# Prompt attention beside the FFN's first part, FFN operand sums woven into the prompt's mixers and output projection, row tiles prepared one ahead

## The chip, the cores and the metric

The kernel runs on one core of a Trainium2 chip. The metric is the device time of one execution in microseconds. A core has TensorE (PE; its weight loads are shown as PEld), VectorE (DVE), ScalarE (ACT), GpSimd (POOL), and queues for transfers, of which SyncE's (SP) carries nearly all here. All matrix products are done on fp32 values split into a high and a low part of type fp32r, with three products (high x high, high x low, low x high) for one.

## The reference

One layer of a hybrid encoder trunk is applied to two sequences with the same weights: the sample (2048 tokens, "s") and the prompt (512 tokens, "p"), 1024 channels each.

```python
h = rms_norm(x, norm1_g)
p = h @ w_in                                   # 1024 -> 1792, split among three mixers
a = windowed_attention(q, k, v, ...)           # 8 heads of 64, 2 kv heads, blocks of 128, +-128 tokens, sink logit
b = multiscale_pool(pool_in, pool_w, pool_scale)   # means over 2/4/8/16 tokens minus token, group linear
c = hyena_mixer(hy_in, ...)                    # short conv, two gated FFT convolutions with implicit filters
cat = concat(rms_norm(a), rms_norm(b), rms_norm(c))
x = x + cat @ w_out
h = rms_norm(x, norm2_g)
u = dwconv3(h @ w_ffn_in, ...)                 # 1024 -> 2 x 2816, depthwise conv of width 3 over tokens
x = x + (gelu(u[..., :2816]) * u[..., 2816:]) @ w_ffn_out
```

## The kernel before

The program is written with a tile framework that inserts the waits and orders the instructions of each engine by its own estimate; the order in which the program issues them is the priority.

Issue order comes from generators. A "main" list and a "side" list of work are run by `drive`: each step of either yields its planned cost in nanoseconds of a planner's clock (`now`). For each cost of main, side may issue work up to `ratio` times that cost. A step that yields `None` waits for a due time (`until`) or for a result (`need`); side then yields to main. `T_NORM` (6500), `T_RMS`, `T_SM` and the like are planned latencies. What is left of side when main is over is issued alone. `weave(x, y)` issues one step of y after each step of x, then the rest of y.

The stages:

1. `front` (main): input projections of both sequences, then the sample's output projection, row tile by row tile (16 of 128 rows), to `x2["s"]` in DRAM. Beside it (side): filter spectra, the sample's pooling, Hyena and attention, then the prompt's attention, then `prep`, which builds `h0`, the normed, transposed and split first 512 rows of the sample (`ffn_prep`, transposes in line 360). Main ends with `need("h0")`.
2. `ffn_in` (main): the FFN's up-projection for these 512 rows, 22 pairs of column tiles, 16 steps of three 128x512 products each (lines 326 to 328, with the weights `fwhi`, `fwlo`). Beside it (side, after `need("up")`): the prompt's pooling and Hyena, its output projection `out_proj`, then `sums(0)` and `sums(1)`. From "up" on, the side work has the banks 4 to 7: attention's scores two (4, 5), its transposes one (6), its output one (7); before, five banks were theirs, two of them for transposes.
3. `ffn_in7` twice: the other 2048 rows in two groups of 1024, as seven products of half-size blocks in place of eight. It needs as operands sums and differences of the two row halves' blocks. `ffn_sums` makes them: per pair of row tiles a load, norm and transposes (line 1329) of two tiles, and sums into a tile `o` (seven blocks), stored to `ops[0]` or `ops[1]` in DRAM. `ffn_operands` loads each of the seven blocks through two `st` buffers, and splits it (ScalarE the high part, VectorE or GpSimd the low part). `sums(0)` takes rows of the sample alone; `sums(1)` pairs the sample's last 512 rows with the prompt's, and waits for each prompt row tile of x2.
4. `ffn_out`: the down-projection of all rows with all weights held in SBUF.

The prompt's `out_proj` works in two halves of 512 columns. In each half it loads that half of `w_out` (eight blocks, scaled and split), and for each of four row tiles loads the concatenated mixers `ca` and the residual, squares, splits and sums (`out_prep`), waits `T_NORM`, and multiplies. The sample's out projection in `front` already uses `out_product`, which does both halves of a row tile in one go.

The functions that the change touches:

Of the kernel before, what the change touches and what calls it, by code (L numbers as in the profile page):

```python
# [11 lines left out]
F32 = mybir.dt.float32  # L12
F32R = mybir.dt.float32r
AF = mybir.ActivationFunctionType
ALU = mybir.AluOpType
# [3 lines left out]
DM = 1024  # L19
KD = DM // 128  # L20
# [209 lines left out]
RATIOS = (1.0, 1.2, 0.8)  # L230
RATIO_P = 1.0
FH = 512
# [3 lines left out]
GROUPS = ((0, 4), (4, 6), (6, 8))  # L236
T_NORM, T_SIN, T_RMS, T_SM, T_PT, T_INV, T_CONV, T_EV, T_POOL, T_LOAD, T_FILL = 6500, 6000, 7000, 9000, 2500, 4500, 9000, 2500, 2500, 4200, 1300
# [5 lines left out]
class Trunk:  # L243
# [51 lines left out]
    def bank(self, i):  # L295
        return self.ps.tile([128, 512], F32, tag=f"b{i}", name=f"b{i}")
# [946 lines left out]
    def out_proj(self, s, bank, src, key):  # L1243

        nc, tc, d = self.nc, self.tc, self.d
        n, L = s.name, s.L
        with tc.tile_pool(name=f"outp{n}", bufs=1, side="right", reuse_waits="tile") as pool:
            for h in range(2):
                hs = slice(h * 512, h * 512 + 512)
                wo = {}  # L1250
                for k in range(KD):
                    raw = pool.tile([128, 512], F32, tag="raw", bufs=2, name="raw")
                    nc.sync.dma_start(out=raw, in_=d["w_out"][0, k * 128:k * 128 + 128, hs])
                    hi, lo = (pool.tile([128, 512], F32R, tag=f"ow{nm}{k}", name=f"ow{nm}{k}") for nm in ("hi", "lo"))
                    go = self.go[:, k:k + 1]
                    nc.scalar.activation(hi, raw, AF.Copy, scale=go)
                    nc.vector.scalar_tensor_tensor(lo, raw, go, hi.bitcast(F32), op0=ALU.mult, op1=ALU.subtract)
                    wo[k] = (hi, lo)
                    if h == 0:
                        yield from self.until(self.now + T_LOAD / 2)  # L1260
                yield from self.need((key, n))
                for t in range(L // 128):
                    ts = slice(t * 128, t * 128 + 128)
                    ca = pool.tile([128, DM], F32, tag="ca", bufs=2, name="ca").rearrange("p (k t) -> p k t", k=KD)
                    nc.sync.dma_start(out=ca, in_=self.cat[n][:, ts].rearrange("(k p) t -> p k t", p=128))
                    x = pool.tile([128, 512], F32, tag="ox", bufs=2, name="ox")
                    nc.sync.dma_start(out=x, in_=src[ts, hs])
                    sq = pool.tile([128, KD, 128], F32, tag="osq", name="osq")
                    hi, lo = (pool.tile([128, KD, 128], F32R, tag=nm, bufs=2, name=nm) for nm in ("chi", "clo"))
                    self.out_prep(ca, sq, hi, lo)  # L1270
                    yield from self.until(self.now + T_NORM)
                    r = self.out_scale(pool, bank, sq, GROUPS)
                    for i, (k0, k1) in enumerate(GROUPS):
                        ps = bank()
                        for k in range(k0, k1):
                            self.mm3(ps, hi[:, k], lo[:, k], wo[k][0], wo[k][1], k == k0, k == k1 - 1)
                            yield 650
                        nc.vector.scalar_tensor_tensor(x, ps, r[:, i:i + 1], x, op0=ALU.mult, op1=ALU.add)
                    nc.gpsimd.dma_start(out=self.x2[n][ts, hs], in_=x)
                    if h:  # L1280
                        self.done.add(("x2", n, t))


    def prep_rows(self, pool, tiles):
# [11 lines left out]
                yield from self.until(t)  # L1296
                yield x

    def ffn_prep(self, tiles, hi, lo, bank):

        with self.tc.tile_pool(name="ffp", bufs=1, side="right", reuse_waits="tile") as pool:
            i = 0
            for x in self.prep_rows(pool, tiles):
                if x is None or isinstance(x, (int, float)):
                    yield x
                    continue
                yield from self.norm_t(x, 128, hi, lo, i * 128, bank)
                i += 1

# [1 line left out]

    def ffn_sums(self, dst, tiles, bank):

        nc = self.nc
        with self.tc.tile_pool(name="ffs", bufs=1, side="right", reuse_waits="tile") as pool:
            i, o = 0, None  # L1320
            for x in self.prep_rows(pool, tiles):
                if x is None or isinstance(x, (int, float)):
                    yield x
                    continue
                pv = []
                for k0 in range(0, KD, 4):
                    ps = bank()
                    for k in range(k0, k0 + 4):
                        nc.tensor.transpose(ps[:, (k - k0) * 128:(k - k0) * 128 + 128], x[:, 128 * k:128 * k + 128], self.ident)  # L1329
                    pv.append(ps.rearrange("p (k t) -> p k t", k=4))  # L1330
                    yield 450
                if i % 2 == 0:
                    o = pool.tile([128, 7, 4, 128], F32, tag="o", name="o")
                    for j in range(2):
                        nc.scalar.activation(o[:, j], pv[j], AF.Copy)
                else:
                    nc.vector.tensor_tensor(o[:, 3], pv[0], o[:, 0], op=ALU.subtract)
                    nc.vector.tensor_tensor(o[:, 4], pv[1], o[:, 3], op=ALU.subtract)
                    nc.scalar.activation(o[:, 2], pv[1], AF.Copy)
                    nc.gpsimd.tensor_tensor(o[:, 5], o[:, 4], o[:, 0], op=ALU.subtract)  # L1340
                    nc.gpsimd.tensor_tensor(o[:, 6], o[:, 1], o[:, 4], op=ALU.subtract)
                    c = i // 2 * 128
                    nc.sync.dma_start(out=dst[:, :, :, c:c + 128].rearrange("p o k t -> p (o k) t"), in_=o.rearrange("p o k t -> p (o k) t"))
                i += 1

    def ffn_operands(self, pool, stage, src):

        h = {}
        for i, op in enumerate((0, 4, 5, 3, 1, 6, 2)):
            x = stage.tile([128, 4, FH], F32, tag="st", bufs=2, name="st")  # L1350
            self.nc.sync.dma_start(out=x, in_=src[:, op])
            h[op] = pool.tile([128, 2, 4, FH], F32R, tag=f"o{op}", name=f"o{op}")
            self.split(x, h[op][:, 0], h[op][:, 1], self.nc.gpsimd if i % 2 else None)
        return h

# [209 lines left out]
    def run(self):  # L1565
        tc, nc, d = self.tc, self.nc, self.d
        S, P = SEQS["s"], SEQS["p"]
        self.done, self.now, self.strict = set(), 0.0, False
        chain = itertools.chain
        c = self.ctx.enter_context(tc.tile_pool(name="const", bufs=1, reuse_waits="tile"))  # L1570
# [3 lines left out]
        def pooled(s, a):  # L1574
            with tc.tile_pool(name="pool" + s.name, bufs=2, side="right", reuse_waits="tile") as pool:
                yield from self.pooling(s, a, pool)
# [12 lines left out]
        att = [att(i) for i in range(3)]  # L1589


        h0 = []

        def prep():

            pool = mctx.enter_context(tc.tile_pool(name="h0", bufs=1, side="right", reuse_waits="tile"))
            h0.extend(pool.tile([128, KD, 512], F32R, name=f"h0{i}") for i in range(2))
            yield from self.ffn_prep([("s", t) for t in range(0, 512, 128)], *h0, a)
            self.done.add("h0")

        def sums(i):

            pairs = [[("s", 512 + t), ("s", 1024 + t)] if i == 0 else [("s", 1536 + t), ("p", t)] for t in range(0, FH, 128)]
            return self.ffn_sums(self.ops[i], [x for p in pairs for x in p], a)

        def consts():
            yield from self.until(START)
# [2 lines left out]
        def pace(r):  # L1610
            self.ratio = r
            return
            yield

        side = chain(consts(), pace(RATIOS[0]), self.spectra(S, a), self.spectra(P, a), pooled(S, a), pace(RATIOS[1]), self.hyena(S, [[0], [1]], a),
                     self.mark("c", "s"), pace(RATIOS[2]), self.attention(S, *att), self.attention(P, *att), prep(), self.need("up"),
                     pooled(P, a), self.hyena(P, [[0, 1]], a), self.mark("cat", "p"),
                     self.out_proj(P, a, d["x_p"][0], "cat"), sums(0), sums(1))

        side = self.drive(chain(self.front(), self.need("h0")), side, RATIO)  # L1620

# [5 lines left out]
        with (tc.tile_pool(name="hops", bufs=1, side="right", reuse_waits="tile") as hops,  # L1627
              tc.tile_pool(name="ffw7", bufs=1, reuse_waits="tile") as pool, tc.tile_pool(name="stage", bufs=1, reuse_waits="tile") as stage):
            fb = self.rotate(range(8))
            for i, parts in enumerate(([(S, 512, 1024)], [(S, 1536, 512), (P, 0, 512)])):  # L1630
                h = self.ffn_operands(hops, stage, self.ops[i])
# [36 lines left out]
```

## Time and profile before

| | |
|---|---|
| median of 3 runs | 3180.19 us (3179.9 to 3184.45) |
| profiled execution | 3178.09 us |
| its span, first to last instruction | 3176.3 us |
| mean granted TensorE clock | 0.98 |
| TensorE busy | 2977.4 us |
| VectorE / ScalarE / GpSimd busy | 1944.5 / 1320.5 / 596.8 us |

Lines "L326" and the like are lines of the program above; a line in a helper (the three products, the split) is shared by many callers, so that tile names tell them apart. Matmuls overlap, so a busy stretch is not necessarily a full one; PEclk is the share of the full clock that TensorE was granted. The span's middle has these marks: the prompt's attention begins at 1074 us, `ffn_in` at 1206 us, its last product is at 1586 us, and `ffn_in7` begins at 1634 us.

### The profile page before, as it was taken

How to read it: one execution, taken by the hardware profiler on the slowest of the kernel's cores; microseconds unless marked ns; L12 is line 12 of the kernel's file. 1: busy time of each engine (PE TensorE's matmuls, PEld its weight loads, DVE VectorE, ACT ScalarE, POOL GpSimd, SP SyncE). 2: the span in 40 equal slices, each digit the busy share in tenths (PEclk: the TensorE clock that was granted, in tenths of full speed). 3: DMA queues.
4: the chain of work that ended last, by engine and by line, in shares of the span. 5: the costliest groups of instructions: out<-in, count | busy, mean ns of one | idle time of the engine just before them, and what ended most of it. 6: DMA issues, size and time to landing. Idle time of an engine off the chain costs nothing.

```text
span 3176.3 us, 41398 instructions
## 1 busy us (share of the span) xinstructions
PE 2977.4 (94%) x15488; PEld 2475.9 (78%) x15488; DVE 1944.5 (61%) x3162; ACT 1320.5 (42%) x2235; POOL 596.8 (19%) x470
## 2 busy tenths in 40 slices
PE   7999999999999978999849999989999999999999
PEld 6888888888888767878637888868888867888887
DVE  7443576769998776665538888887777642111111
ACT  5223444458876554443433444444444432111110
POOL 1000000022242310011243444443233200000000
PEclk9999999999999998999969999999999999999999
DMA  5555576654433335654872222232222154223222
GB/s 176 149 154 145 163 214 188 184 157 117 132 106 95 118 107 159 197 180 140 241 216 93 80 80 80 83 123 88 84 81 80 61 168 146 73 73 100 73 74 76
DMA packets 438990, 401.40 MB, mean 126 GB/s; under 512 B 75961, under 2 KB 369465, under 8 KB 435973
## 3 DMA queue, kind: packets, MB, share of 16 engines
q1 hardware_dynamic: 435557, 388.10, 40.8%
q0 software_dynamic: 2944, 10.49, 0.8%
q8 instruction: 122, 2.00, 0.3%
q14 instruction: 79, 0.65, 0.1%
q10 hardware_dynamic: 288, 0.16, 0.0%
HBM read 294.86 MB, written 103.81 MB: 126 GB/s over the span
## 4 chain that ended last, share of the span: by engine, by line
PE 47%; DMA 4%; DVE 2%; issue 1%; ACT 1%; POOL 1%; SPq 0%; DVEq 0%; POOLq 0%; ACTq 0%
PE b L328 16%; PE b L326 16%; PE b L327 16%; DMA rw<-in_w_ffn_out_dram 2%; DVE cv L1436 1%; DMA st<-ops 1%; DMA raw<-in_w_out_dram 1%; DMA ops<-o 1%; DMA fw<-in_w_ffn_in_dram 0%; POOL o L321 0%; DVE wo L321 0%; DMA nx<-x2s 0%; ACT wo L320 0%; DVE cv L1441 0%; PE b L1329 0%
## 5 line engine op out<-in xcount | busy, mean ns | idle before, releaser
L326 PE MATMUL b<-o,fk 128*128 128x512 f32 x1056 | 419.7, 398 | 12.5 <-ACT o L320 12.1
L327 PE MATMUL b<-o,fk 128*128 128x512 f32 x1056 | 419.9, 398 | 10.1 <-DVE o L321 8.6
L328 PE MATMUL b<-o,fk 128*128 128x512 f32 x1056 | 419.0, 397 | 0.0
L326 PE MATMUL b<-wo,ah 128*128 128x512 f32 x880 | 349.2, 397 | 7.8 <-ACT wo L320 6.9
L327 PE MATMUL b<-wo,ah 128*128 128x512 f32 x880 | 348.7, 396 | 0.8 <-DVE wo L321 0.8
L328 PE MATMUL b<-wo,al 128*128 128x512 f32 x880 | 348.8, 396 | 0.3
L321 DVE TENSOR_TENSOR al<-ar,ah 128x512 fp32r<-128x512 f32 x110 | 75.8, 691 | 406.2 <-ACT ah L320 406.2
L1436 DVE SCALAR_TENSOR_TENSOR cv<-u,cst,cv 128x1024 f32<-128x1024 f32 (+2 forms) x264 | 308.4, 1208 | 11.5 <-ACT cv L1434 7.7
L320 ACT ACTIVATE ah<-ar 128x512 fp32r<-128x512 f32 x110 | 69.4, 631 | 457.5 <-PE b L327 457.4
L326 PEld LDWEIGHTS b<-o,fk 128*128 128x128 f32 x1056 | 199.7, 189 | 62.7 <-ACT o L320 13.6
L327 PEld LDWEIGHTS b<-o,fk 128*128 128x128 f32 x1056 | 199.8, 189 | 61.0 <-DVE o L321 10.6
L328 PEld LDWEIGHTS b<-o,fk 128*128 128x128 f32 x1056 | 199.4, 189 | 47.9
L1400 DVE TENSOR_TENSOR u<-b,u 128x512 f32<-128x512 f32 x220 | 151.2, 687 | 132.2 <-PE b L328 129.3
L326 PE MATMUL b<-W,h 128*128 128x256 f32 (+1 forms) x672 | 225.6, 336 | 1.4 <-ACT o L510 0.6
L327 PE MATMUL b<-W,h 128*128 128x256 f32 (+1 forms) x672 | 215.6, 321 | 0.7 <-DVE W L321 0.3
L328 PE MATMUL b<-W,h 128*128 128x256 f32 (+1 forms) x672 | 214.6, 319 | 0.0
L326 PEld LDWEIGHTS b<-wo,ah 128*128 128x128 f32 x880 | 165.5, 188 | 50.5 <-ACT wo L320 7.8
L326 PE MATMUL b<-h,W 128*128 128x256 f32 x640 | 200.7, 314 | 3.5 <-ACT W L320 1.6
L328 PEld LDWEIGHTS b<-wo,al 128*128 128x128 f32 x880 | 165.5, 188 | 42.5 <-DVE al L321 2.3
L327 PEld LDWEIGHTS b<-wo,ah 128*128 128x128 f32 x880 | 165.5, 188 | 41.8 <-DVE wo L321 1.6
L328 PE MATMUL b<-h,W 128*128 128x256 f32 x640 | 184.6, 288 | 2.8 <-DVE W L321 2.8
L1389 POOL TENSOR_TENSOR fs<-fw 128x512 f32<-128x512 f32 x44 | 89.3, 2029 | 505.1 <-DMA fw<-in_w_ffn_in_dram 333.7
(228 smaller groups left out, 6758.6 us busy)
## 6 DMA issues: line engine op xcount, KB each, us to landing
fw<-in_w_ffn_in_dram SPq DMA_DIRECT2D x132, 512.0 KB, 3.8
ar<-acts SPq DMA_DIRECT2D x88, 256.0 KB, 2.8
nx<-in_x_sample_dram SPq DMA_DIRECT2D x32, 512.0 KB, 4.8
tf<-in_t2f_s_dram SPq DMA_DIRECT2D x64, 256.0 KB, 3.4
ops<-o SPq DMA_DIRECT2D x8, 1792.0 KB, 8.6
st<-ops SPq DMA_DIRECT2D x14, 1024.0 KB, 6.3
raw<-in_w_in_dram SPq DMA_DIRECT2D x44, 256.0 KB, 3.0
acts<-cv SPq DMA_DIRECT2D x22, 512.0 KB, 4.2
```

The source lines that it names most:

```text
L320: self.keep(nc.scalar.activation(hi, x, AF.Copy))
L321: self.keep((engine or nc.vector).tensor_tensor(lo, x, hi.bitcast(F32), op=ALU.subtract))
L326: nc.tensor.matmul(ps, lhsT=lhi, rhs=rhi, start=start, stop=False, skip_group_check=more)
L327: nc.tensor.matmul(ps, lhsT=lhi, rhs=rlo, start=False, stop=False, skip_group_check=more)
L328: nc.tensor.matmul(ps, lhsT=llo, rhs=rhi, start=False, stop=stop, skip_group_check=more)
L1389: nc.gpsimd.tensor_tensor(s12[:, 0:4], a21, a22, op=ALU.add)
L1400: nc.vector.tensor_tensor(o, ps, x, op=ALU.add)
L1436: nc.vector.scalar_tensor_tensor(o, u[:, part, c + i - 1:c + i - 1 + k], self.fcw[:, i, m:m + 1], o, op0=ALU.mult, op1=ALU.add)
```

## The change

- `prep` follows the sample's attention directly. The prompt's attention moves behind `need("up")`, to stage 2, at the head of the side list.
- In stage 2, one pool `ffs` for both sums stays open. Attention, pooling and Hyena of the prompt are woven with `sums(0)`; `out_proj` of the prompt is woven with `sums(1)`. `ffn_prep` and `ffn_sums` get their pool from outside; their bodies stay.
- `out_proj` loads all of `w_out` once in blocks of 1024 columns, through the two buffers ("ox") that it shares with the residual rows, and does each row tile once, with `out_product`; tile t + 1 is loaded and prepared before the products of tile t.
- `ffn_operands` allocates the seven operand tiles ahead, in the reverse of the order in which they are filled.

```diff
 def out_proj(self, s, bank, src, key):
-            for h in range(2):
-                ... (w_out blocks of 512 columns, need, then for each row tile: load, out_prep,
-                     until(now + T_NORM), out_scale, products of this half, store of this half)
+            wo = {}
+            for k in range(KD):
+                raw = pool.tile([128, DM], F32, tag="ox", bufs=2, name="raw")
+                nc.sync.dma_start(out=raw, in_=d["w_out"][0, k * 128:k * 128 + 128, :])
+                hi, lo = (pool.tile([128, DM], F32R, name=f"ow{nm}{k}") for nm in ("hi", "lo"))
+                go = self.go[:, k:k + 1]
+                nc.scalar.activation(hi, raw, AF.Copy, scale=go)
+                nc.vector.scalar_tensor_tensor(lo, raw, go, hi.bitcast(F32), op0=ALU.mult, op1=ALU.subtract)
+                wo[k] = (hi, lo)
+                yield from self.until(self.now + T_LOAD / 2)
+            yield from self.need((key, n))
+            def prep(t):
+                ...
+                return self.out_prep(ca, sq, hi, lo) + (x, self.now + T_NORM)
+            nxt = prep(0)
+            for t in range(L // 128):
+                hi, lo, sq, x, at = nxt
+                yield from self.until(at)
+                r = self.out_scale(pool, bank, sq, GROUPS)
+                if t + 1 < L // 128:
+                    nxt = prep(t + 1)
+                yield from self.out_product(bank, hi, lo, x, r, GROUPS, wo)
+                nc.gpsimd.dma_start(out=self.x2[n][t * 128:t * 128 + 128, :], in_=x)
+                self.done.add(("x2", n, t))
 def ffn_operands(self, pool, stage, src):
-        h = {}
-        for i, op in enumerate((0, 4, 5, 3, 1, 6, 2)):
+        h, order = {}, (0, 4, 5, 3, 1, 6, 2)
+        for op in order[::-1]:
+            h[op] = pool.tile([128, 2, 4, FH], F32R, tag=f"o{op}", name=f"o{op}")
+        for i, op in enumerate(order):
             x = stage.tile([128, 4, FH], F32, tag="st", bufs=2, name="st")
             self.nc.sync.dma_start(out=x, in_=src[:, op])
-            h[op] = pool.tile([128, 2, 4, FH], F32R, tag=f"o{op}", name=f"o{op}")
             self.split(x, h[op][:, 0], h[op][:, 1], self.nc.gpsimd if i % 2 else None)
 def run(self):
+        def prompt():
+            yield from self.need("up")
+            with tc.tile_pool(name="ffs", bufs=1, side="right", reuse_waits="tile") as pool:
+                yield from self.weave(chain(self.attention(P, *att), pooled(P, a), self.hyena(P, [[0, 1]], a), self.mark("cat", "p")),
+                                      sums(0, pool))
+                yield from self.weave(self.out_proj(P, a, d["x_p"][0], "cat"), sums(1, pool))
         side = chain(consts(), ..., self.hyena(S, [[0], [1]], a),
-                     self.mark("c", "s"), pace(RATIOS[2]), self.attention(S, *att), self.attention(P, *att), prep(), self.need("up"),
-                     pooled(P, a), self.hyena(P, [[0, 1]], a), self.mark("cat", "p"),
-                     self.out_proj(P, a, d["x_p"][0], "cat"), sums(0), sums(1))
+                     self.mark("c", "s"), pace(RATIOS[2]), self.attention(S, *att), prep(), prompt())
```

More of the change, by code (lines that the diff above doesn't have):

```diff
@@ L1247, in out_proj @@
         with tc.tile_pool(name=f"outp{n}", bufs=1, side="right", reuse_waits="tile") as pool:
-            for h in range(2):
[L1249 to L1281, printed above, removed]
@@ new lines, in out_proj @@
+            yield from self.need((key, n))
+            def prep(t):
+                ts = slice(t * 128, t * 128 + 128)
+                ca = pool.tile([128, DM], F32, tag="ca", name="ca").rearrange("p (k t) -> p k t", k=KD)
+                nc.sync.dma_start(out=ca, in_=self.cat[n][:, ts].rearrange("(k p) t -> p k t", p=128))
+                x = pool.tile([128, DM], F32, tag="ox", bufs=2, name="ox")
+                nc.sync.dma_start(out=x, in_=src[ts, :])
+                sq = pool.tile([128, KD, 128], F32, tag="osq", name="osq")
+                hi, lo = (pool.tile([128, KD, 128], F32R, tag=nm, bufs=2, name=nm) for nm in ("chi", "clo"))
+                return self.out_prep(ca, sq, hi, lo) + (x, self.now + T_NORM)
@@ L1297, in prep_rows @@
                 yield x
[L1299 to L1316, printed above, removed]
-        nc = self.nc
[L1319 to L1344, printed above, removed]
@@ new lines, in ffn_prep, with ffn_sums @@
+    def ffn_prep(self, pool, tiles, hi, lo, bank):
+        i = 0
+        for x in self.prep_rows(pool, tiles):
+            if x is None or isinstance(x, (int, float)):
+                yield x
+                continue
+            yield from self.norm_t(x, 128, hi, lo, i * 128, bank)
+            i += 1
+    def ffn_sums(self, pool, dst, tiles, bank):
+        nc = self.nc
+        i, o = 0, None
+        for x in self.prep_rows(pool, tiles):
+            if x is None or isinstance(x, (int, float)):
+                yield x
+                continue
+            pv = []
+            for k0 in range(0, KD, 4):
+                ps = bank()
+                for k in range(k0, k0 + 4):
+                    nc.tensor.transpose(ps[:, (k - k0) * 128:(k - k0) * 128 + 128], x[:, 128 * k:128 * k + 128], self.ident)
+                pv.append(ps.rearrange("p (k t) -> p k t", k=4))
+                yield 450
+            if i % 2 == 0:
+                o = pool.tile([128, 7, 4, 128], F32, tag="o", name="o")
+                for j in range(2):
+                    nc.scalar.activation(o[:, j], pv[j], AF.Copy)
+            else:
+                nc.vector.tensor_tensor(o[:, 3], pv[0], o[:, 0], op=ALU.subtract)
+                nc.vector.tensor_tensor(o[:, 4], pv[1], o[:, 3], op=ALU.subtract)
+                nc.scalar.activation(o[:, 2], pv[1], AF.Copy)
+                nc.gpsimd.tensor_tensor(o[:, 5], o[:, 4], o[:, 0], op=ALU.subtract)
+                nc.gpsimd.tensor_tensor(o[:, 6], o[:, 1], o[:, 4], op=ALU.subtract)
+                c = i // 2 * 128
+                nc.sync.dma_start(out=dst[:, :, :, c:c + 128].rearrange("p o k t -> p (o k) t"), in_=o.rearrange("p o k t -> p (o k) t"))
+            i += 1
@@ L1597, in prep, with sums @@
             h0.extend(pool.tile([128, KD, 512], F32R, name=f"h0{i}") for i in range(2))
-            yield from self.ffn_prep([("s", t) for t in range(0, 512, 128)], *h0, a)
+            with tc.tile_pool(name="ffp", bufs=1, side="right", reuse_waits="tile") as pool:
+                yield from self.ffn_prep(pool, [("s", t) for t in range(0, 512, 128)], *h0, a)
             self.done.add("h0")
-        def sums(i):
+        def prompt():
[4 more added lines that the diff above has]
+                yield from self.weave(self.out_proj(P, a, d["x_p"][0], "cat"), sums(1, pool))
+        def sums(i, pool):
             pairs = [[("s", 512 + t), ("s", 1024 + t)] if i == 0 else [("s", 1536 + t), ("p", t)] for t in range(0, FH, 128)]
-            return self.ffn_sums(self.ops[i], [x for p in pairs for x in p], a)
+            return self.ffn_sums(pool, self.ops[i], [x for p in pairs for x in p], a)
         def consts():
```

## The prediction

> **What bounds the kernel now.** I read the page first (busy shares and 40 slices), then the table by stretches of time, then TensorE's waits in the two stretches that stand out, then the order of time there.
>
> ```profile
> span 3176.3 us, 41398 instructions
> ...
> PE 2977.4 (94%) x15488; PEld 2475.9 (78%) x15488; DVE 1944.5 (61%) x3162; ACT 1320.5 (42%) x2235; POOL 596.8 (19%) x470
> ...
> PE   7999999999999978999849999989999999999999
> ...
> PEclk9999999999999998999969999999999999999999
> ```
>
> TensorE is busy for 94% of the span, so only its idle time (199 us) and the time at a low granted clock can be won. Slices 15 and 21 are the holes. The stretches around them:
>
> ```profile
> core 0: us, PE busy (x) PEld busy (x) DVE busy (x) ACT busy (x) POOL busy (x), PEclk, DMA share, GB/s
> 1074.00:1172.00 98.00, 89.14 (x459) 72.13 (x458) 78.34 (x220) 58.17 (x144) 30.85 (x34) 0.98 0.31 95
> 1100.00:1160.00 60.00, 55.89 (x302) 45.42 (x301) 53.98 (x172) 45.12 (x120) 15.64 (x18) 1.00 0.18 56
> 1172.00:1206.00 34.00, 9.77 (x44) 7.72 (x43) 15.86 (x22) 13.86 (x22) 2.83 (x5) 0.59 0.53 168
> 1206.00:1340.00 134.00, 129.56 (x694) 108.59 (x693) 88.82 (x156) 55.88 (x84) 0.00 (x0) 0.99 0.61 177
> 1340.00:1500.00 160.00, 159.00 (x708) 128.61 (x707) 100.44 (x161) 68.64 (x83) 30.43 (x49) 1.00 0.53 166
> 1500.00:1586.00 86.00, 73.57 (x336) 59.12 (x335) 50.03 (x76) 37.72 (x60) 19.83 (x20) 0.94 0.81 238
> 1586.00:1634.00 48.00, 11.17 (x51) 8.82 (x49) 21.43 (x26) 17.75 (x27) 22.82 (x19) 0.59 0.77 223
> 1634.00:1720.00 86.00, 70.40 (x263) 52.98 (x264) 52.85 (x42) 34.31 (x38) 30.17 (x12) 0.91 0.45 150
> ```
>
> First column busy against length: 1172 to 1206 and 1586 to 1634 are nearly empty (24.2 and 36.8 us idle, clock 0.59); 1500 to 1586 loses 12.4, 1634 to 1720 loses 15.6; the prompt's attention (1074 to 1172) loses 8.9; pooling and Hyena 4.4; the output projection 1.0. What TensorE waits for, first in 1074 to 1206, then in 1500 to 1720:
>
> ```profile
> PE b L360 <- DVE ss L347: 17.5, 1, 17.5
> PE b L360 <- DVE nx L350: 5.5, 2, 4.7
> ...
> PE b L1329 <- DVE nx L350: 22.1, 7, 11.6
> PE b L1329 <- DVE ss L347: 19.3, 4, 9.8
> PE b L326 <- ACT o L320: 12.1, 3, 7.9
> ```
>
> L360 is the transpose of `prep` (the FFN's first operand h0), L1329 that of `ffn_sums`. Both are chains of load, norm, transpose with nothing beside them: h0 because it stands behind the prompt's attention in the side list, the sums because they stand last. In order of time:
>
> ```profile
> 1074.25 0.43 SPq L1034 DMA_DIRECT2D bias<-in_bias_dram  x1
> ...
> 1171.03 0.39 PE L328 MATMUL b<-wo,h 128*128 128x512 f32 x1
> ...
> 1174.10 1.99 ACT L320 ACTIVATE fwhi<-fw 128x1024 fp32r<-128x1024 f32 x2
> ...
> 1183.66 0.90 SPq L338 DMA_DIRECT2D nx<-x2s  x2
> ...
> 1206.30 1.65 PE L326 MATMUL b<-h,fwhi 128*128 128x512 f32 x3
> ...
> 1209.98 0.40 PE L328 MATMUL b<-h,fwlo 128*128 128x512 f32 x1
> ...
> 1210.21 0.40 PE L326 MATMUL b<-h,fwhi 128*128 128x512 f32 x1
> ```
>
> The prompt's attention begins at 1074 with its bias; the front's last product is at 1171; the FFN's first weights are split from 1174; h0's rows are only fetched at 1183; the FFN starts at 1206. Products of 512 columns start 0.233 us apart (last two rows), so a planner step of three is 0.70 us.
>
> **The change part by part.** The sum is made against the profiled execution (3178.1 us, span 3176.3 and 1.8 around it), 2.1 us below the median.
>
> *Step 1, h0 before the prompt's attention.* From 1074, when the sample's attention has been issued, the front still has to do:
>
> ```profile
> L326 PE MATMUL b<-W,h 128*128 128x512 f32 x54 | 22.9, 424 | 0.0
> ...
> L326 PE MATMUL b<-wo,h 128*128 128x512 f32 x20 | 8.1, 407 | 0.0
> ...
> L360 PE MATMUL b<-cst,nx 128*128 128x128 f32 x31 | 7.6, 424 | 23.1 <-DVE ss L347 17.5 <-DVE nx L350 5.5
> ```
>
> 74 steps x 0.70 = 52 us of products. `prep` took 1183 to 1206, 23 us bare; beside 52 us of products it is hidden. On SP its g2 and eight row transfers now go ahead of the attention's loads and stores instead of behind them; nothing of the front's waits for those. "up" then comes near 1074 + 52 + 5 (its 32 transposes) + 4 (last product to first split weights, 1171 to 1175) = 1135, not 1206. Of the 34 us in 1172 to 1206, about 2 are attention's, 5 the transposes at full clock and 4 stay: **23 us are won**. Without that cover it costs 23 again.
>
> *Step 2, attention moved beside the FFN's first part.* Its TensorE work, 89.1 - 52 = 37 us, moves and is neutral. Its stretch before loses 8.9 us; that goes, and a new loss comes. The FFN loads VectorE as the front did; VectorE is at 54.0 of 60 in 1100 to 1160, TensorE at 55.9. Into it are now woven eight rows of sums(0):
>
> ```profile
> L350 DVE SCALAR_TENSOR_TENSOR nx<-nx,rr,g 128x1024 f32<-128x1024 f32 x60 | 79.0, 1316 | 40.6 <-POOL rr L349 39.3 <-DMA g<-in_norm_g_dram 1.1
> ...
> L1338 DVE TENSOR_TENSOR o<-b,o 128x512 f32<-128x512 f32 x4 | 2.8, 692 | 0.4
> ```
>
> 8 x 1.32 + 4 x 2 x 0.69 = 16 us more on VectorE. And ScalarE alternates Exp with Gelu:
>
> ```profile
> L1127 ACT ACT_TABLE_LOAD x1 | 1.3, 1283 | 0.0
> L1470 ACT ACT_TABLE_LOAD x1 | 1.3, 1283 | 1.7 <-DVE pd L998 1.7
> ```
>
> Now one load precedes all 160 Exp groups and one all 22 Gelu; Copy, Square and Identity between them cause none. Beside attention, in at most 111 steps (below; 16 to a Gelu), some 7 Gelu fall between its 8 groups of Exp: up to 14 loads x 1.283 = 18 us, on a ScalarE that is at 45.1 of 60 there. The Trainium skill (ScalarE: Activation LUTs, "Table sets: the hidden batching unit") says to batch by set and speaks against this step; its figure of about 2.7 us with the drain would make that some 38 us by an estimate, and the sum below some 10 us worse. The trace agrees that a change of function costs a load, with 1.283, and that decides. Also, after "up" attention has one bank for its transposes instead of two. The new loss lies between 0 (all hidden in a longer mix) and 34 (16 + 18, nothing hidden); the row nearest is 1100 to 1160 with 7%, so over about 107 us (85 steps of 0.70 from step 3, the 37, some 10 of transposes) 7 us, plus a share of the added work: I take **15; won 8.9 - 15 = -6**.
>
> *Step 3, sums(0) and sums(1) woven, one row tile ahead in the output projection.* The main list has 352 steps; those beside each side stage are the counts of L327 in 1206 to 1340, of L327 in 1340 to 1500, and of L328 after:
>
> ```profile
> L327 PE MATMUL b<-h,fwhi 128*128 128x512 f32 x112 | 45.2, 404 | 0.0
> ...
> L327 PE MATMUL b<-h,fwhi 128*128 128x512 f32 x156 | 61.8, 396 | 0.0
> ...
> L328 PE MATMUL b<-h,fwlo 128*128 128x512 f32 x86 | 35.2, 409 | 0.0
> ```
>
> Pooling and Hyena go with 112 steps, the output projection with 156, and the sums with 86, after which sums(1) stands bare. In the new text the projection waits T_NORM (6.5 units) once instead of eight times: 16.8 + 6.5 + 64 x 0.7 + 16 x 0.5 = 76 units (the planner's thousand), or 117 steps of 0.65. With 112, and 12 for the last row of sums(1), 111 steps are left for attention. It went with 74 steps in the front at ratio 0.8, so 59 at 1.0 plus 12 for sums(0), perhaps 85 with its waits. So the side list should end some 25 steps (18 us) before the main one, and the sums cost no bare time. The eight loads of w_out become 512 KB on two shared buffers; they are planned 2.1 us apart and land slower (3.7 us for 256 KB in the row below), so the first products may come up to 15 us late, covered by the FFN's 111 to 117 steps.
>
> What is late next is the operand change to `ffn_in7`. It cannot vanish:
>
> ```profile
> st<-ops SPq DMA_DIRECT2D x14, 1024.0 KB, 6.3
> ...
> raw<-in_w_out_dram SPq DMA_DIRECT2D x32, 256.0 KB, 3.7
> ```
> ```profile
> 2060.00:2140.00 80.00, 64.47 (x255) 50.89 (x254) 72.08 (x59) 38.52 (x42) 37.42 (x14) 0.91 0.38 125
> 1587.13 1.07 PE L1329 MATMUL b<-cst,nx 128*128 128x128 f32 x8 [0.57 <-DVE nx L350]
> ...
> 1613.52 1.94 PE L1329 MATMUL b<-cst,nx 128*128 128x128 f32 x8 [11.64 <-DVE nx L350]
> ```
>
> The second change of operands, where everything has long been in DRAM, still loses 15.5 us. Now 1500 to 1720 loses 64.9 idle, plus low clock: eight transposes take 1.94 instead of 1.07 (about 5 us over the sums), and some 30 products after 1634 at about half pace (6 us): 76. What stays is at least 15.5, at most 15.6 + 8 (first load and split bare) + 15 (last sums row bare) = 39; I take **26: won 50**. The reversed allocation of the o tiles only lets o0, o4 and o5 lie where the projection was, not where h0 lies: part of that 26.
>
> *Small edits at nothing:* `out_prep` four times instead of eight, 12 one-column products fewer, `ca` loads halved: the stretch 1340 to 1500 is full at 159 of 160. SP gets the sums' loads and 1.8 MB stores earlier; a load of x2p waits on SP for POOL's store, with weight loads of the FFN behind it, which have two buffers. If that cover is gone, a few us for each of four rows.
>
> Sum: 23 - 6 + 50 = **67 us: 3178 - 67 = 3111**, against the median 3113; I write 3112. A measurement here tells 0.2% (6 us) from no change.
>
> **The rivals.** (a) *Everything hidden:* attention costs no more than the 8.9 it did, the change to `ffn_in7` the 15.5 of the second one plus 4 of clock: 23 + 0 + 56 = 79, and up to 88 where attention loses nothing: 3090 to 3099. For it: 111 steps against 71. Against: VectorE at 90%.
> (b) *Attention binds ScalarE and VectorE:* 34 us lost and the end of the sums bare: 23 - 25 + 37 = 35: 3143. For it: the table loads, one bank. Against: the FFN's products may run ahead in the list.
> (c) *Slower:* with one bank, transpose, ScalarE's copy and VectorE's difference of each block of probabilities go in series, and attention takes over twice its steps. Then the side list outlasts the main one and the prompt's Hyena and projection waits stand bare. Losing 23 + 50 needs over 70 us of bare waits: 3190. It decides from about 200 steps for attention. Against it: 74 steps before, with VectorE as full.
> (d) *No move:* the scheduler orders by its own costs, and h0 or the sums stay late: 3170 to 3185.
>
> **How the numbers follow.** Forecast (3103 to 3125) 0.48, (a) 0.22, (b) 0.19, (c) 0.06, (d) 0.05. Faster: the first three and a little of (d), 0.90; within 0.2%: most of (d), 0.04; slower: 0.06. The range leaves out (c), (d) and the far ends of (a) and (b): 3082 to 3146.
>
> **What would show it.** Right: the first `fwhi` product near 1135; no idle before L360; L1329's waits under 10 us; ten or more table loads; idle at the change to `ffn_in7` about 20 us. Wrong: TensorE below 85% beside attention, or sums' transposes after the last `fwlo` product.

## The result and the profile after

The changed kernel takes 3129.55 us (median, 3126.43 to 3130.31) against 3180.05 us (3172.3 to 3184.45) before: ratio 0.9842, 95% interval 0.9822 to 0.9862. The forecast was 3112 with a range of 3082 to 3146. The profiled executions differ by 49.0 us (3178.1 and 3129.1), where the sum had said 67. One of the four executions with the old allocation, below, took 4132.22 us at a granted clock of 0.653; its ratio is that of the other three.

The page of the changed kernel, first part:

```profile
span 3127.4 us, 41184 instructions
...
PE 2966.7 (95%) x15464; PEld 2464.4 (79%) x15464; DVE 1942.1 (62%) x3138; ACT 1320.5 (42%) x2229; POOL 595.4 (19%) x446
...
PE   7999999999999998999869999979999999999999
...
PEclk9999999999999999999989999989999999999999
```

The hole of slice 15 is gone; that of slice 21 is still there, but shallower (busy 6 tenths of the slice, where it was 4). TensorE's idle time fell from 198.9 to 160.7 us (span less busy), its busy time by 10.7. The table by stretches (same columns as before: length, then the busy time of PE, PEld, DVE, ACT and POOL, clock, DMA share, GB/s) has one row each for the front's rest, attention, pooling and Hyena, the output projection with `sums(1)`, the operand change, and the first part of `ffn_in7`:

```profile
1074.00:1137.00 63.00, 60.87 (x293) 48.91 (x292) 39.24 (x65) 18.26 (x29) 18.87 (x31) 1.00 0.50 169
1137.00:1294.00 157.00, 142.91 (x700) 112.86 (x701) 126.39 (x285) 117.61 (x224) 36.01 (x28) 0.99 0.62 178
1294.00:1422.00 128.00, 122.96 (x647) 102.79 (x647) 84.44 (x146) 51.85 (x78) 0.00 (x0) 0.96 0.63 180
1422.00:1580.00 158.00, 142.06 (x624) 111.50 (x622) 88.97 (x131) 57.39 (x76) 35.77 (x39) 0.97 0.64 200
1580.00:1598.00 18.00, 0.49 (x1) 0.49 (x2) 7.23 (x7) 9.54 (x8) 6.54 (x2) 0.57 0.65 218
1598.00:1640.00 42.00, 32.71 (x121) 24.48 (x121) 31.51 (x20) 16.62 (x18) 26.30 (x13) 0.86 0.49 163
```

First column less PE busy is the idle time: 2.1, 14.1, 5.0, 15.9, 17.5 and 9.3 us, 63.9 in all. The rows of before gave 8.9 + 24.2 + 4.4 + 1.0 + 12.4 + 36.8 + 15.6 = 103.3 for the same work. So 39.4 of the 49.0 us are idle time of TensorE here, and the busy time, 10.7 lower over the whole span, accounts for the rest, within 1 us. In order of time, the marks are these:

```profile
1138.03 0.50 PE L326 MATMUL b<-h,fwhi 128*128 128x512 f32 x1 [1.25 <-ACT fwhi L320]
...
1293.72 0.58 SPq L1150 DMA_DIRECT2D catp<-ob  x1
...
1563.15 0.52 SPq L1339 DMA_DIRECT2D ops<-o  x1
...
1579.55 0.40 PE L328 MATMUL b<-h,fwlo 128*128 128x512 f32 x1
...
1590.00 1.05 SPq L1381 DMA_DIRECT2D fw<-in_w_ffn_in_dram  x2
...
1597.51 0.79 PE L326 MATMUL b<-o,fk 128*128 128x512 f32 x1 [17.56 <-ACT fk L320]
```

"Up" comes 68 us earlier (1138 against 1206), the prompt's attention stores its last block at 1294, the last sums go out at 1563, the FFN's first part ends at 1580, `ffn_in7` begins at 1598 (1634 before). What TensorE waited for, first beside attention, then beside the projection, then ScalarE's own wait over both:

```profile
PE b L1114 <- ACT o L1331: 5.7, 3, 3.6
...
PE b L326 <- ACT o L1331: 5.9, 2, 3.4
PE b L1325 <- DVE nx L350: 4.9, 3, 3.1
...
ACT o L1331 <- DMA ops<-o: 26.5, 5, 11.7
```

L1331 is ScalarE's copy of the even row tile into `o`. There is one `o`, so the copy waits until the store of the last pair has landed (up to 11.7 us), and ScalarE stands idle in front of it for 26.5 us in all. TensorE's two waits end with that copy.

### The profile page after: what moved, and what is told of

Its sections match the earlier page's. It is cut to its first block, busy times and chain, and to the rows that moved or that the text cites. A ratio compares the mean times of both kernels' runs of the same rounds, so it can differ in the third digit from the quotient of the medians.

```text
span 3127.4 us, 41184 instructions
## 1 busy us (share of the span) xinstructions
PE 2966.7 (95%) x15464; PEld 2464.4 (79%) x15464; DVE 1942.1 (62%) x3138; ACT 1320.5 (42%) x2229; POOL 595.4 (19%) x446
## 4 chain that ended last, share of the span: by engine, by line
PE 46%; DVE 1%; issue 1%; POOL 1%; DMA 1%; ACT 1%; SPq 0%; POOLq 0%; DVEq 0%
PE b L327 15%; PE b L326 15%; PE b L328 15%; DMA st<-ops 0%; DVE cv L1438 0%; DVE cv L1433 0%; POOL o L321 0%; ACT o L320 0%; DVE o L321 0%; POOL fs L1386 0%; DMA rw<-in_w_ffn_out_dram 0%; ACT cv L1431 0%; POOL fs L1388 0%; POOL fs L1387 0%; ACT fk L320 0%
## 5 line engine op out<-in xcount | busy, mean ns | idle before, releaser
L1433 DVE SCALAR_TENSOR_TENSOR cv<-u,cst,cv 128x1024 f32<-128x1024 f32 (+2 forms) x264 | 304.3, 1193 | 12.3 <-ACT cv L1431 8.4
```

What stands on the lines that cost most here:

```text
L1433: nc.vector.scalar_tensor_tensor(o, u[:, part, c + i - 1:c + i - 1 + k], self.fcw[:, i, m:m + 1], o, op0=ALU.mult, op1=ALU.add)
```

## The experiments

Ratios are to the kernel before, measured on the same chip in the same stretch of time; 0.001 is about 3.2 us.

| kernel | median, us | ratio | 95% interval |
|---|---|---|---|
| changed kernel once more | 3128.56 | 0.9849 | 0.9829 to 0.9869 |
| `o` split | 3134.71 | 0.9869 | 0.9851 to 0.9887 |
| `sums(1)` not woven | 3128.47 | 0.9847 | 0.9828 to 0.9865 |
| attention in front | 3154.97 | 0.9932 | 0.9913 to 0.9951 |
| old projection | 3139.5 | 0.9885 | 0.9862 to 0.9907 |
| old allocation | 3129.04 | 0.985 | 0.9825 to 0.9876 |
| no Gelu | 3123.72 | 0.9844 | 0.9829 to 0.9858 |
| weights first | 3125.7 | 0.9846 | 0.9832 to 0.986 |
| nothing woven | 3148.56 | 0.9904 | 0.9885 to 0.9922 |
| nothing woven, old projection | 3179.46 | 1.0009 | 0.9994 to 1.0024 |
| `sums(1)` not woven, weights first | 3129.52 | 0.985 | 0.9832 to 0.9867 |

### The changed kernel once more

No edit.

> The changed kernel once more, as the measure for the runs beside it on the same chip. Every theory: about 3130 us, 1.6% below before; idle of TensorE 14 us beside attention, 16 us in the projection's stretch, 27 us at the change to ffn_in7.

0.9849, as in the result. The profiled execution of this one took 13.5 us less in its span (3113.9) than the one shown above. The FFN's first part, first in the one above and then in this one:

```profile
1138.00:1580.00 442.00, 407.93 (x1968) 327.15 (x1968) 299.80 (x562) 225.86 (x376) 71.53 (x66) 0.97 0.63 187
```
```profile
1136.00:1566.00 430.00, 402.89 (x1967) 324.22 (x1968) 299.91 (x562) 226.39 (x376) 71.50 (x66) 0.98 0.64 192
```

The same products took 5 us less busy time and 7 us less idle time. So idle sums of single profiles are read below with some 7 us of play; the ratios carry the verdicts.

### `o` split in two

```diff
-                o = pool.tile([128, 7, 4, 128], F32, tag="o", name="o")
+                o = pool.tile([128, 2, 4, 128], F32, tag="oa", bufs=2, name="oa")
...
+                q = pool.tile([128, 5, 4, 128], F32, tag="ob", name="ob")
```
The two blocks that the even row tile fills get two buffers, the other five one, each with its store; the squares' scratch of the sums' norm is bf16 to make room.

> The sums' tile o is split in two: the two blocks that the next pair writes first (L1331) get two buffers, the other five one; the room comes from a bf16 tile for the unused squares of the norm. Theory A (ScalarE's copy L1331 waits for the 1.8 MB store of the pair before, 26.6 us in all, and holds two of the four banks, so that TensorE waits 11.6 us for it): the wait for the store goes, TensorE's idle time falls from 16 to 8-10 us in the projection's stretch and from 14 to 9 beside attention, 8 to 12 us faster than e0_same. Rival B (the stretch is limited by the chain of load, norm and transpose itself, or by w_out's arrival, and another wait takes the place of this one): within 4 us of e0_same.

0.9869: no gain. TensorE's waits over the FFN's first part, then by time the stretch of attention and the whole first part:

```profile
PE b L1325 <- DVE nx L350: 9.4, 3, 4.5
PE b L1163 <- DVE qs L1095: 3.6, 2, 3.4
PE b L328 <- DVE fwlo L321: 3.5, 2, 2.9
...
PE b L1114 <- ACT oa L1331: 0.7, 1, 0.7
```
```profile
1137.00:1296.00 159.00, 142.75 (x669) 112.67 (x670) 119.08 (x273) 114.90 (x220) 36.47 (x27) 0.94 0.58 168
...
1137.00:1590.00 453.00, 416.54 (x1968) 335.23 (x1968) 297.07 (x562) 226.39 (x376) 68.74 (x66) 0.95 0.61 182
```

The wait for the copy is gone (0.7 in place of 5.7 + 5.9), and the idle time is still 36.5 us: waits for the sums' normed rows, for attention's queries and for FFN weights stand where it stood. The stretch of attention loses 16.3 us, no less than the 14.1 with the wait. So the wait that the profile names was not what the stretch costs. That others were due almost as late would fit, but it is not shown; what sets the sum of them was not settled.

### `sums(1)` not woven

```diff
-                yield from self.weave(self.out_proj(P, a, d["x_p"][0], "cat"), sums(1, pool))
+                yield from self.out_proj(P, a, d["x_p"][0], "cat")
+                yield from sums(1, pool)
```

> sums(1) behind the prompt's output projection instead of woven into it; all else as changed. Theory A (the weaving of the sums is worth what stood bare before, less the 15 us of waits that it brings into the projection's stretch): the projection's stretch falls to under 6 us idle, the sums' transposes come at or behind the last product of ffn_in with 20 to 40 us of waits, and the time is 15 to 30 us above 3130. Rival E (the weave costs as much as it brings): within 6 us of 3130.

0.9847, the same. Its projection alone, its `sums(1)` and the operand change:

```profile
1417.00:1511.00 94.00, 91.14 (x395) 72.60 (x394) 56.77 (x82) 32.49 (x36) 19.52 (x25) 0.98 0.53 171
1511.00:1567.00 56.00, 48.28 (x231) 38.32 (x229) 31.06 (x47) 23.65 (x37) 12.40 (x13) 0.97 0.77 240
1567.00:1586.00 19.00, 0.46 (x2) 0.27 (x2) 6.28 (x8) 7.21 (x8) 2.81 (x2) 0.61 0.67 196
```

Unwoven, the projection is nearly full (2.9 us idle) and the sums lose 7.7: 10.6 against 15.9 woven. The sums' last store comes at 1574, 7 us after the last `fwlo` product, and the change takes 1 us more. The second weave costs as much in scattered waits as it saves.

### Attention back in front

```diff
-self.attention(S, *att), prep(), prompt())
+self.attention(S, *att), self.attention(P, *att), prep(), prompt())
```
and the first weave without attention.

> The prompt's attention back in the front, ahead of h0; all else as changed. Theory A (steps 1 and 2 of the prediction: 23 us won, 5 lost beside attention): h0 is bare again, 34 us with TensorE nearly empty, and the time is 15 to 20 us above 3130. Rival F (attention beside the FFN eats up the gain, since the side list then fills the main one): within 6 us of 3130, with over 50 us of ffn_in left after the last sums.

0.9932, some 26 us slower than the changed kernel (0.9932 less 0.9849, times 3178), more than the 15 to 20 expected. By time, h0 bare; pooling and Hyena woven with `sums(0)`; and the end of the FFN's first part, where the last sums go out at 1528:

```profile
1172.00:1209.00 37.00, 11.49 (x54) 9.10 (x53) 22.50 (x40) 14.84 (x24) 3.73 (x5) 0.58 0.65 215
1209.00:1375.00 166.00, 146.43 (x750) 122.98 (x749) 101.64 (x166) 70.34 (x111) 15.32 (x17) 0.90 0.73 208
...
1513.00:1607.00 94.00, 93.82 (x406) 75.28 (x404) 48.87 (x75) 33.17 (x42) 3.35 (x4) 1.00 0.47 147
```

The 25.5 us of idle time before the FFN are back. A second cost comes with it: with attention gone, `sums(0)` has only pooling and Hyena to be woven with, which now lose 19.6 us instead of 5.0, while the FFN's products have no side work beside them from 1528 to 1607.

### The old output projection

The function `out_proj` of the kernel before, in two halves of columns, woven with `sums(1)`.

> The prompt's output projection as before (two halves of 512 columns, eight waits of T_NORM, none ahead), woven with sums(1); all else as changed. Theory A (side list ends some 17 us before the main one, and the old projection is some 60 steps, 40 us, longer in the planner's clock): it outlasts the main list by 20 us or more, and the time is 12 to 30 us above 3130. Rival G (one tile ahead is worth nothing, since the main list covers it): within 6 us.

0.9885, some 11 us slower than the changed kernel, just short of the 12 to 30 expected. The operand change and TensorE's longest wait beside the projection:

```profile
1575.00:1600.00 25.00, 2.43 (x11) 1.60 (x9) 7.07 (x9) 8.18 (x10) 3.04 (x3) 0.57 0.72 234
```
```profile
PE b L1222 <- DVE oss L1223: 7.8, 3, 4.1
```

The side list now ends after the main one: the last sums go out at 1588.6, 13.5 us after the last `fwlo` product (20 or more were expected), and TensorE stands for 22.6 us instead of 17.5. The 86 us behind it lose 13.4 us instead of 9.3.

### The old order of allocation

```diff
-        for op in order[::-1]:
-            h[op] = pool.tile([128, 2, 4, FH], F32R, tag=f"o{op}", name=f"o{op}")
```
with each tile allocated after its load's issue, as before.

> The operand tiles of ffn_in7 allocated one by one in the order of use, as before; all else as changed. Theory A (in the changed kernel the first split of an operand comes at 1580.7, after ffn_in's last product at 1579.7, so that the place of the tiles cannot matter much): 0 to 4 us slower than 3130. Rival H (the place lets the first operands in early): 8 us slower or more, with the first split behind 1585.

0.985: no difference.

### No Gelu in the FFN's first part

```diff
-                    nc.scalar.activation(cv, cv, AF.Gelu)
+                    nc.scalar.activation(cv, cv, AF.Copy)
```
In `ffn_in` alone; the Gelu is left out there.

> ffn_in leaves Gelu out (Copy stands in its place), so that ScalarE changes its function table no more beside attention. Theory A (table loads cost little: TensorE's waits beside attention name other things): some ten loads of 1.283 us fewer, 13 us of ScalarE, and within 4 us of e0_same. Rival C (ScalarE at 75% is the bound of that stretch, as the page's rule has it): idle beside attention falls by 5 us or more, and the time by 5 to 13 us.

0.9844, 1.6 us under the changed kernel and well within the intervals. The changed kernel's table loads, then this one's mark for the end of attention:

```profile
L1467 ACT ACT_TABLE_LOAD x6 | 7.7, 1283 | 1.1 <-DVE cv L1463 0.7 <-DVE edge L1464 0.4
L1130 ACT ACT_TABLE_LOAD x4 | 5.1, 1283 | 0.1
L1127 ACT ACT_TABLE_LOAD x2 | 2.6, 1283 | 0.0
```
```profile
1278.22 0.58 SPq L1150 DMA_DIRECT2D catp<-ob  x1
```

Without the loads attention ends 143 us after the first `fwhi` product (1134.9) instead of 156, and the kernel ends no sooner: attention sets the end of nothing while FFN steps are left. Nor did TensorE's idle time beside attention fall clearly: 12.3 us without the loads, 14.1 and 10.7 in the two profiles of the changed kernel. The Trainium skill (ScalarE: Activation LUTs, "Table sets: the hidden batching unit") says to batch activations by set. Its rule holds for ScalarE's own time here and did not reach the kernel's.

### The first weights of `ffn_in7` first

```diff
+                first = self.fw7(pool, 0)
                 h = self.ffn_operands(hops, stage, self.ops[i])
```
The first two weight tiles are loaded on SP ahead of the operand blocks.

> The first two weight tiles of ffn_in7 are loaded ahead of the seven operand blocks in program order. Theory A (at the change to ffn_in7 TensorE waits 17.6 us for the first weights' split, whose loads stand on SP behind block loads that wait for a free buffer): the loads are issued at about 1586 instead of 1590, and the change costs 4 to 5 us less; 3125 us against 3130. Rival D (the seven operand splits on ScalarE, VectorE and GpSimd set the time): the first product comes earlier, but waits later for the operands, and the time stays within 2 us.

0.9846: no difference that can be told. The change and what follows it:

```profile
1579.00:1592.00 13.00, 0.04 (x1) 0.00 (x0) 5.26 (x6) 7.25 (x6) 5.17 (x1) 0.60 0.60 197
1592.00:1674.00 82.00, 70.95 (x275) 54.52 (x276) 64.23 (x47) 35.23 (x41) 44.72 (x20) 0.90 0.41 139
```

The first product comes 5 us sooner after the last one, and the 82 us behind it lose 11.1 us, where the first profile of the changed kernel lost 9.3 (82.00 less 72.71). Their loads were issued at 1584.7 instead of 1590.0. So of the 17.5, some 5 us were the weights queued on SP behind operand blocks; some 2 us of it are lost again behind the change.

### Nothing woven, with the new and with the old projection

```diff
-                yield from self.weave(chain(self.attention(P, *att), ...), sums(0, pool))
-                yield from self.weave(self.out_proj(P, a, d["x_p"][0], "cat"), sums(1, pool))
+                yield from chain(self.attention(P, *att), ...)
+                yield from self.out_proj(P, a, d["x_p"][0], "cat")
+                yield from chain(sums(0, pool), sums(1, pool))
```
The second kernel also has the old `out_proj`, so that of the change only the moves of `prep` and attention are left (and the order of allocation, which made no difference).

> Neither sums(0) nor sums(1) is woven: both follow the new output projection, one after the other; all else as in the kernel after. With sums(1) alone unwoven the time did not move, and 56 of the FFN's 352 steps still lay beside it. Theory A: what hides the sums is the number of FFN steps left beside them, not the weaving as such. Attention then takes about 132 steps, pooling and Hyena 95, the projection 60; 65 are left, enough for sums(0), and most of sums(1) stands bare at some 12 us a pair: 25 to 45 us slower than the kernel after (3153 to 3175), and TensorE idle for over 30 us between the last fwlo product and the first product of ffn_in7. Rival B: the order of issue hardly matters because the engines' queues run ahead; within 6 us of the kernel after.

> h0 first and attention beside the FFN as in the kernel after, but the old output projection in two halves and both sums behind it, as before. Theory A (steps beside the sums decide): attention 132 steps, mixers 95 and the old projection's 150 are 377 against 352, so the projection's tail and all eight pairs of the sums stand bare, some 12 us each: 80 to 110 us slower than the kernel after (3208 to 3238), which is slower than the kernel before by 30 to 60. Rival B (each part brings its own term, 23 - 6 for h0 and attention): 3160 to 3165, faster than before by 15 to 20.

New projection: 0.9904, some 17 us slower than the changed kernel: between the two expectations, the first one's direction with its size too large. Old projection: 1.0009, the time of the kernel before. It is 51 us slower than the changed kernel, not 80 to 110, and neither theory's time came. By time, first the new projection (attention, projection, the sums beside the FFN, the sums bare), then the old (attention, projection, the sums bare, `ffn_in7`):

```profile
1133.00:1278.00 145.00, 140.19 (x671) 110.46 (x672) 117.58 (x274) 103.58 (x199) 20.69 (x13) 1.00 0.40 116
...
1396.00:1484.00 88.00, 85.10 (x379) 68.56 (x378) 54.13 (x79) 30.74 (x34) 14.95 (x24) 1.00 0.54 172
1484.00:1547.00 63.00, 55.54 (x276) 44.34 (x274) 39.57 (x58) 29.02 (x46) 16.89 (x17) 1.00 0.81 246
1547.00:1599.00 52.00, 11.92 (x51) 9.50 (x49) 26.44 (x30) 20.48 (x33) 20.76 (x18) 0.56 0.83 257
```
```profile
1139.00:1293.00 154.00, 148.91 (x700) 117.49 (x701) 124.52 (x288) 106.32 (x203) 20.33 (x13) 0.99 0.41 117
...
1401.00:1526.00 125.00, 121.51 (x539) 98.13 (x538) 79.90 (x130) 53.38 (x65) 30.95 (x47) 0.99 0.52 163
...
1545.00:1638.00 93.00, 23.13 (x97) 18.83 (x97) 38.80 (x48) 32.08 (x54) 38.52 (x34) 0.58 0.82 247
1638.00:1720.00 82.00, 67.63 (x239) 50.97 (x239) 49.88 (x37) 31.17 (x32) 29.93 (x12) 0.86 0.45 151
```

Attention alone beside the FFN loses 4.8 and 5.1 us, less than the 8.9 it lost in the front, and the projection alone 2.9 and 3.5. What is bare at the end, the change included, loses 40.1 and 69.9. `ffn_in7` of the second begins where it did before (1638 against 1634): what h0 won was paid back at the end.

Together with the changed kernel and the one with the old projection these are four kernels that differ in two things: neither new projection nor weaving 1.0009; projection alone 0.9904, 33 us better; weaving alone 0.9885, 39 us; both 0.9849, 51 us. They do not add, since each hides the same bare sums: 69.9, 40.1, 22.6 and 17.5 us of idle time at the end, in this order.

### `sums(1)` not woven and weights first

Both edits above.

> sums(1) behind the projection and the first two weight tiles of ffn_in7 loaded ahead of the operand blocks. Theory A: both small gains add, some 5 us less idle in the projection's stretch and 4 at the operand change: 3117 to 3121. Rival B: with the sums ending 7 us after the last fwlo product, the operand blocks and not the weights come last, and the time stays within 4 us of the kernel after (3124 to 3132).

0.985: the two edits together gave no gain either, and no kernel here with the whole computation beats the changed kernel by more than the intervals. Its projection's stretch, its change, and `ffn_in7` after:

```profile
1421.00:1571.00 150.00, 141.48 (x626) 112.89 (x624) 88.40 (x130) 56.74 (x73) 31.27 (x37) 0.97 0.63 197
1571.00:1590.00 19.00, 0.13 (x1) 0.13 (x1) 6.15 (x8) 7.20 (x8) 2.81 (x2) 0.58 0.67 195
1590.00:1672.00 82.00, 66.35 (x246) 49.98 (x247) 56.18 (x43) 32.92 (x36) 42.82 (x19) 0.89 0.43 143
```

The change takes 18.9 us, and 15.7 are lost behind it. With `sums(1)` alone unwoven the first weights already stood ahead of the operand blocks on SP (issued from 1574.5, the blocks from 1580.9), so here the second edit had nothing to move.

## Why the prediction was right, and where it was off

The measured time, 3129.55, lies in the range but 4 us above the band that the prediction took as likeliest (3103 to 3125), on the side of rival (b). The way was right, and its signs came: h0 early, ten more table loads, the sums' transposes done before the last `fwlo` product, some 20 us idle at the change.

**Step 1, h0 first (23 won).** Right in place and size beside its neighbours: the first `fwhi` product came at 1138, 1135 was expected, and L360 waits 1.2 us. But the 23 us are not this step's own. With the moves alone the kernel takes the time of before (1.0009): the step frees TensorE early, and the sums then stand bare for longer. Nor are the 50 us of step 3 its own: with attention in front, so without steps 1 and 2, the kernel won only 22 us (0.9932). The moves alone win nothing, the rest alone 22, both together 48. The prediction let steps 1 and 3 add; the runs show that step 1 is kept only where step 3 makes room at the end.

**Step 2, attention beside the FFN (15 lost).** The sum was right, 14.1 measured (10.7 in the second profile), the reason only in part. Attention by itself loses 5 us there; the other 6 to 9 came with `sums(0)`. The profile names the copy into the one `o` for 5.7 of them, but with that wait gone the stretch lost no less, so what of `sums(0)` costs them stays open. The table loads came as counted, ten more than before, and without them the time stayed. The step count failed more: attention was to take 85 FFN steps. Products with `fwlo` count them, per stretch of the table above (attention, pooling and Hyena, projection up to the sums' last store, rest; a product across a border counts on both sides):

```profile
L328 PE MATMUL b<-h,fwlo 128*128 128x512 f32 x141 | 57.1, 405 | 0.5 <-DVE fwlo L321 0.5
...
L328 PE MATMUL b<-h,fwlo 128*128 128x512 f32 x97 | 40.7, 419 | 0.0
...
L328 PE MATMUL b<-h,fwlo 128*128 128x512 f32 x91 | 37.3, 410 | 0.0
...
L328 PE MATMUL b<-h,fwlo 128*128 128x512 f32 x25 | 9.9, 397 | 0.0
```

Attention took 141, pooling and Hyena 97 instead of 112, the projection with `sums(1)` 91 instead of 117 + 12. The errors cancelled: 25 steps were left, as forecast. Working out planner steps from another stage at another ratio, and adding up planned delays in units, were both poor guides; that the end came out was luck.

**Step 3, the sums (50 won).** The operand change was to keep 26 us; it keeps 17.5 + 9.3 = 26.8 of idle time. The slow products behind it, some 6 us in the sum, did not all go: 121 of them were busy for 32.7 us, where 0.233 for each would be 28.2. The sums' transposes wait 8.6 us in all over the FFN's first part, where they waited 41.4 at the end of it before. The term that was mis-sized is the one costed at nothing, the projection's stretch "full at 159 of 160": woven with `sums(1)` it loses 15.9 us (13.7 in the second profile), 14.9 more than before. That is nearly the whole distance between 67 and 49. TensorE's waits there name the copy into `o` (5.9), the sums' normed rows (4.9) and the squares of `out_prep` (2.5); how much each of them costs is not shown, since the stretch lost 14.5 with the first one gone. The prediction named a cover for the added work but no price for the weave in this stretch; unwoven, the same projection loses 2.9, and the sums behind it 7.7. The weave's own worth is therefore small where the sums still fit behind the projection (`sums(1)`: nothing), and 17 us for both together, after paying some 22 us of scattered waits (14.1 + 15.9 against 4.8 + 2.9).

**The rivals.** (a) was right that the bare stretches would go, all but the change itself, and failed on the woven stretches' 30 us. (b) did not come: attention took 156 us where the sum had about 107, but the sums did not stand bare, and attention 12 us shorter left the time the same. (c) came within reach in the experiment with the moves alone, at 141 steps for attention, not 200: with the old projection nothing is won. (d) did not come.

## What to carry to other kernels

Side work that stands bare at the end can be hidden by weaving it into earlier work or by making the work ahead of it shorter; two edits that hide the same bare work do not add, and a move that only frees time earlier is worth nothing until the end is filled, so price them together. A weave is not free: the woven stages here lost some 6 to 15 us more than without their partner. Taking away the longest named wait of one weave gained nothing, so a named wait is not yet the price of the weave. And count steps beside a stage in that stage.

## What the runs showed of the hardware

The granted clock fell to half while TensorE was busy, in the changed kernel's Hyena stretch:

```profile
1344.00:1348.00 4.00, 3.16 (x25) 3.05 (x24) 2.54 (x6) 1.26 (x3) 0.00 (x0) 0.88 0.66 138
1348.00:1352.00 4.00, 4.00 (x21) 4.00 (x20) 0.67 (x2) 0.00 (x0) 0.00 (x0) 0.50 0.74 193
1352.00:1356.00 4.00, 4.00 (x15) 3.52 (x15) 2.07 (x5) 2.44 (x5) 0.00 (x0) 0.50 0.52 153
```

The only idle time in the 12 us ahead of it is 0.84 us, behind runs of 64-column products. The Trainium skill (TensorE: Matmul & The Clock Gate, "HAM oscillation — how this bites in real kernels") asks for no gaps over about 3.4 us; these rows show a drop after a much shorter one. The second execution of the same program has no such spell at that place; others, near 44 and 376 us, come in both. They fit the 5 us of busy time by which two executions of the same program differ above (clock 0.97 and 0.98), and the 13.6 us that the same products took longer with `o` split (416.5 against 402.9, clock 0.95 against 0.98). Whether the narrow products cause them was not tried.
